# The first stage of a hybrid backbone block: one load of x, one chain for both norms, the shift from two extra columns

## The chip, the cores and the metric

One core of one Trainium2 chip runs the whole block as one program. The metric is device time in microseconds (us), the median of several executions. TensorE (PE) multiplies, VectorE (DVE), ScalarE (ACT) and GpSimd (POOL) do element work, and SyncE (SP) issues most of the loads.

## The reference

A hybrid block over 1024 latent tokens and 256 context tokens of width 1024, one layer deep. What matters for this case is its beginning:

```python
s_lat, s_ctx = jax.nn.silu(c), jax.nn.silu(c_ctx)
mod_l = (s_lat @ w_mod[l] + b_mod[l])[:, None, :]
mod_c = s_ctx @ w_mod[l] + b_mod[l]
sh1, sc1, g1, sh2, sc2, g2 = jnp.split(mod_l, 6, axis=-1)
csh1, csc1, cg1, csh2, csc2, cg2 = jnp.split(mod_c, 6, axis=-1)
u_lat = _modulate(_rmsnorm(x, norm1_g[l]), sh1, sc1)
u_ctx = _modulate(_rmsnorm(ctx, norm1_g[l]), csh1, csc1)
...
rgx_l, rgg_l, mlx_l, mlo_l, gr_l, gm_l = jnp.split(u_lat @ w_in, splits, axis=-1)
xm_l, q_l, k_l, v_l, gin_l = _mlstm_inputs(_to_col_major(mlx_l, rows), ml_conv_w, ml_conv_b, ml_wq, ml_wk, ml_wv)
```

After that come two recurrent branches (RG-LRU and mLSTM, in both directions), a gated merge, a second modulated norm, a SwiGLU and a last norm; none of that is changed.

## The kernel before

The kernel keeps channels on the 128 partitions, so x is eight tiles of 128 x 1024 (channel tile k, all tokens) and the context eight of 128 x 256. Every product with a weight is done in three matmuls, because each factor is split into a high part (`wh`, `ah`) and a low part (`wl`, `al`): wh x ah, wh x al, wl x ah (`gemm`, L106). A weight tile `wr` is loaded by SP; POOL makes `wh` (L94), DVE makes `wl` (L97). For 1024 tokens each matmul comes twice, 512 columns each.

The modulation is a matrix product of its own. `mod_a(i, ...)` multiplies the activated conditioning vector `s` by the tile `wm` number i (L282) and ACT copies the result to `mo` (L285). `mod_b` turns it into columns with `sel` (L292), DVE adds the bias into `modc` (L293), and for tiles 8 to 15, the scale, computes the factor `a1` (L297). Tiles 0 to 7 are the shift.

The first stage, block `p0`, computes the first four output blocks m = 0 to 3 of the part `mlx` of the input projection for the latent tokens. It doesn't wait for the norm. For m = 0 and 1 (the *first pass*) it multiplies x times `a1` without norm and shift: `un_h` and `un_lo` make the two parts of tile k, `part(k, (0, 1))` the 12 matmuls, `un_sq` adds the squares of tile k to `accl`. Then `rms_cols` sums `accl` over the channels (`prms`, L143) and takes the inverse root (`rstd_cols`, L132 to L137, six short operations), and `bcast_col` spreads it over the partitions with PE (`rbl`, L152); the result is `rb`. `put_latent` (L222) copies the accumulators `pg` of blocks 0 and 1 to `X`, POOL multiplies them by `rb` (L445), and ACT adds the shift (L449). The shift's share, `shw`, is the product of the weight with the shift column of `modc`: 16 matmuls of one column (`psh`, L411).

For m = 2 and 3 (the *second pass*) `normed` (L330, L331) makes the normed and shifted tile and `normed_low` (L335) its low part; `part(k, (2, 3))` multiplies. The order of k is 5, 6, 7, 0, 1, 2, 3, 4 here, as five buffers hold x: tiles 5 to 7 are still there, and 0 to 4 are loaded a second time. Within this pass ACT squares the context tiles, POOL adds them up (`accc`, L307), and a second `rms_cols` and `rbc` make the context's norm. DVE then scales the context (L451), ACT makes `ch`, DVE `cl` (L454).

Block `p1` follows: `context(m)` multiplies `ch` and `cl` for block m into `pc`, ACT copies it into `X` ahead of the latent tokens (L510), and DVE runs the convolution over `X`.

All instructions of `p0` on PE, ACT, DVE and POOL stand in a hand-written order: the code's order is the engine's order (`tc.manual_schedule`). SP's loads go out in the order of their calls, at most eight at a time, each when its buffer is free. The order in `p1` is made by a scheduler. `s_s`, the activated conditioning vector, is stored to DRAM by POOL at the start (L232) for use by a row much later (L999); the store writes its 1024 elements one by one.

Of the kernel before, what the change touches and what calls it, by code (L numbers as in the profile page):

```python
# [15 lines left out]
T = 1024  # L16
# [12 lines left out]
MPP = 4  # L29
ENG4 = {mybir.EngineType.PE, mybir.EngineType.Activation, mybir.EngineType.DVE, mybir.EngineType.Pool}  # L30
# [11 lines left out]
def hybrid_block(ctx, tc, xT, ctxT, vec, gbias, wmod, wmt, win, wbr, wbm, wo, wfi, wfo, qkvt, wif, rgw,  # L42
# [160 lines left out]
    ch = uc.tile([128, KT, TC], F32R, name="ch")  # L203
    cl = uc.tile([128, KT, TC], F32R, name="cl")
# [3 lines left out]
    with pool("p1g", bufs=2, space=PSUM) as pg_, pool("p1s", bufs=3, space=PSUM) as ps_, \  # L208
# [15 lines left out]
        with pool("p0") as p0:  # L224
# [7 lines left out]
            nc.gpsimd.dma_start(s_s.rearrange("o (k p) -> p (o k)", p=128), s2[:, :, 0])  # L232
# [10 lines left out]
            x_sb, c_sb = {}, {}  # L243

            def load_mod(*idx):
                for i in idx:
                    wms[i] = p0.tile([128, KT, 128], F32, tag="wm", name="wm", bufs=4)
                    nc.sync.dma_start(wms[i], wmod[i])

            def load_x(k):  # L250
                x_sb[k] = p0.tile([128, T], F32, tag="x", name="x", bufs=5)
                nc.sync.dma_start(x_sb[k], xT[:, k])

            def load_c():
                for j in range(2):
                    t_ = p0.tile([128, KT, 128], F32, tag="wm", name="wm", bufs=4).rearrange("p (a b) c -> p a (b c)", b=2)
                    nc.sync.dma_start(t_, ctxT[:, 4 * j:4 * j + 4])
                    for k in range(4):
                        c_sb[4 * j + k] = t_[:, k]

            accl, sqx = [p0.tile([128, T], F32, name=n) for n in ("accl", "sqx")]
            accc = p0.tile([128, TC], F32, name="accc")
            rb = p0.tile([128, T], F32, name="rb")
            shw = p0.tile([128, 2], F32, name="shw")
# [35 lines left out]
            def ctx_sums():  # L300
                for k in range(KT):
                    if k == 0:
                        nc.scalar.activation(accc, c_sb[0], AF.Square)
                    else:
                        sq = p0.tile([128, TC], F32, tag="sqc", name="sqc", bufs=2)
                        nc.scalar.activation(sq, c_sb[k], AF.Square)
                        nc.gpsimd.tensor_tensor(accc, accc, sq, op=ALU.add)  # L307

            KB = (5, 6, 7, 0, 1, 2, 3, 4)

            def part(k, ms):
                for m in ms:
                    gemm(wfirst[m], halves(pgs[m], uh, ul), [k], *((0, 7) if m < 2 else (KB[0], KB[-1])))

# [7 lines left out]
            def un_sq(k):  # L322
                sq = accl if k == 0 else (rb, sqx)[k % 2]
# [14 lines left out]
            with tc.manual_schedule(engines=ENG4):  # L338
                pgs = [pg_.tile([128, 2, 512], F32, tag="g", name="pg") for _ in range(2)]
# [9 lines left out]
                load_mod(14, 15)  # L349
                un_h(1)  # L350
                un_lo(1)
                wfirst[1][2]()
                un_sq(0)
                load_x(5)
                mod_b(10, 11)
                part(0, (0, 1))
                un_h(2)
                un_lo(2)
                un_sq(1)
                load_x(6)  # L360
                part(1, (0, 1))
# [3 lines left out]
                un_sq(2)  # L365
                load_x(7)
                part(2, (0, 1))
                mod_b(12, 13)
                load_mod(4, 5, 6, 7)
                un_h(4)  # L370
                un_lo(4)
                part(3, (0, 1))
                mod_a(14, 15)
                wfirst.append(load_split(win[18], late=True))
                un_sq(3)
                mod_b(14, 15)
                un_h(5)
                un_lo(5)
                un_sq(4)
                part(4, (0, 1))  # L380
                un_h(6)
                un_lo(6)
                un_sq(5)
                mod_a(4, 5, 6, 7)
                load_mod(0, 1, 2, 3)
                part(5, (0, 1))
# [12 lines left out]
                mod_a(0, 1, 2, 3)  # L399
                load_c()  # L400
# [11 lines left out]
                normed_low(5)  # L412
                normed(6)
                load_x(2)
                normed_low(6)
                load_x(3)
                xs01 = [new_x() for _ in range(2)]
                for m in range(2):
                    put_latent(xs01[m], pgs[m])
                for m in range(2):  # L420
                    pgs.append(pg_.tile([128, 2, 512], F32, tag="g", name="pg"))
                wfirst[3][2]()
                for i, k in enumerate(KB):
                    if i + 2 < KT:
                        normed(KB[i + 2])
                    if i + 1 < KT and i > 0:
                        normed_low(KB[i + 1])
                    if i == 1:
                        load_x(4)
                    if i == 1:  # L430
                        ctx_sums()
                    if i == 0:
                        nc.vector.tensor_copy(shw, psh[:, 0:2])
                    part(k, (2, 3))
                    if i == 3:
                        yc = rms_cols(p0, pc_.tile([128, 512], F32, tag="c", name="prms"), accc, 2)
                    if i == 6:
                        rbc = ps_.tile([128, 512], F32, tag="s", name="rbc")
                        for c in range(2):
                            bcast_col(p0, yc[:, c:c + 1], rbc[:, c * 128:c * 128 + 128])  # L440
                    if i in (1, 3):
                        m = (i - 1) // 2
                        X = xs01[m]
                        xv = X[:, 261:1285].rearrange("p (w r) -> p w r", r=16)
                        nc.gpsimd.tensor_tensor(xv, xv, rb.rearrange("p (r w) -> p w r", r=16), op=ALU.mult)  # L445
                    if i in (5, 6):
                        m = i - 5
                        X = xs01[m]
                        nc.scalar.activation(X[:, 261:1285], X[:, 261:1285], AF.Identity, bias=shw[:, m:m + 1])  # L449
                for k in range(KT):  # L450
                    nc.vector.scalar_tensor_tensor(c_sb[k], c_sb[k], a1[:, k, 1:2], rbc[:, 0:TC], op0=ALU.mult, op1=ALU.mult)  # L451
# [6 lines left out]
        with pool("p1") as p1:  # L458
# [15 lines left out]
            prev = None  # L474

# [1034 lines left out]
```

## Time and profile before

| what | value |
|---|---|
| median of three executions (lowest to highest) | 1910.63 us (1910.33 to 1914.82) |
| the profiled execution's own time | 1913.69 us |
| its span, first to last instruction | 1911.9 us |
| mean granted clock of TensorE | 0.991 |
| PE busy | 1847.2 us, 97% |
| DVE, ACT, POOL busy | 64%, 32%, 18% |
| second pass, first matmul to first context matmul | 72.10 to 105.44 us |

A clock of 1.00 is TensorE's full level, 2.4 GHz, and 0.50 the lower one, 1.2 GHz. A timeline row merges instructions of one kind that follow each other: its start, the time from the first one's start to the last one's end, what they are, and in brackets how long the engine was idle before and whose work ended the idleness. Each fp32 matmul of the modulation, of `psm`, `prms`, `rbl` and `psh` counts as two passes. The DMA share is the mean busy share of 16 DMA engines, and it can pass 1 where several packets of an engine overlap.

### The profile page before, as it was taken

What the parts mean: (1) busy time and instruction counts of PE and PEld (TensorE: products, weight loads), DVE (VectorE), ACT (ScalarE), POOL (GpSimd) and SP (SyncE); (2) the same over time, 40 slices, a digit from 0 to 9 for tenths busy, and PEclk for the clock granted to TensorE, in tenths of its full rate; (3) what the DMA queues carried; (4) which work ended last, traced back from release to release, by engine and by line L of the source; (5) the groups of instructions that cost most, each with busy time, mean ns of one, the idle gap of its engine ahead of it and who ended that gap; (6) DMA issues with size and microseconds to landing.
All of it is one profiled execution on the core that took longest, in us unless ns stands there. A gap on an engine that the chain in (4) does not pass through costs nothing.

```text
span 1911.9 us, 23058 instructions
## 1 busy us (share of the span) xinstructions
PE 1847.2 (97%) x8878; PEld 1520.5 (80%) x8878; DVE 1230.9 (64%) x1887; ACT 610.0 (32%) x842; POOL 348.0 (18%) x452
## 2 busy tenths in 40 slices
PE   6799999999999999999999999999999999999997
PEld 4678778888877878788888888778888888888886
DVE  4676558888716474747776446787755555587755
ACT  3433256767422222222310112443333333210013
POOL 0311111111116151515101013220000000110003
PEclk9899999999999999999999999999999999999998
DMA  9432211212260515150796444343322222653102
GB/s 269 153 141 114 91 53 51 65 50 68 100 187 21 166 25 163 26 162 13 253 346 236 145 150 140 105 143 133 132 85 86 78 83 100 222 176 107 56 1 88
DMA packets 89989, 228.83 MB, mean 120 GB/s; under 512 B 8056, under 2 KB 37272, under 8 KB 89752
## 3 DMA queue, kind: packets, MB, share of 16 engines
q1 hardware_dynamic: 77160, 183.28, 30.0%
q0 software_dynamic: 11888, 43.54, 5.9%
q8 instruction: 70, 1.15, 0.3%
q10 hardware_dynamic: 832, 0.53, 0.1%
q14 instruction: 39, 0.32, 0.1%
HBM read 177.42 MB, written 49.91 MB: 119 GB/s over the span
## 4 chain that ended last, share of the span: by engine, by line
PE 89%; DVE 6%; ACT 1%; DMA 1%; issue 1%; POOL 1%; SPq 0%; DVEq 0%; ACTq 0%
PE pg L110 11%; PE pg L112 11%; PE pg L114 11%; PE pp L1122 7%; PE pp L1124 7%; PE pp L1123 7%; PE pp L1334 4%; PE pp L1336 4%; PE pp L1335 4%; PE po L891 3%; PE pC L896 3%; PE po L889 2%; PE po L110 2%; PE po L112 2%; PE po L114 2%; DMA wm<-in_wmod 1%
## 5 line engine op out<-in xcount | busy, mean ns | idle before, releaser
L110 PE MATMUL pg<-ah,wh 128*128 128x512 f32 x896 | 284.6, 398 | 4.6 <-ACT X L222 3.5
L112 PE MATMUL pg<-al,wh 128*128 128x512 f32 x896 | 282.7, 396 | 5.4 <-DVE al L335 5.4
L114 PE MATMUL pg<-ah,wl 128*128 128x512 f32 x896 | 280.6, 394 | 1.6 <-DVE wl L97 1.6
L94 POOL TENSOR_SCALAR wh<-wr 128x1024 fp32r<-128x1024 f32 x102 | 114.3, 1124 | 597.2 <-PE pg L112 217.5
L97 DVE TENSOR_TENSOR wl<-wr,wh 128x1024 fp32r<-128x1024 f32 x102 | 126.6, 1243 | 120.1 <-POOL wh L94 119.5
L112 PEld LDWEIGHTS pg<-al,wh 128*128 128x128 f32 x896 | 165.4, 190 | 39.9 <-DVE al L335 6.2
L110 PEld LDWEIGHTS pg<-ah,wh 128*128 128x128 f32 x896 | 165.4, 191 | 37.9 <-issue 5.6
L114 PEld LDWEIGHTS pg<-ah,wl 128*128 128x128 f32 x896 | 165.7, 189 | 36.9 <-DVE wl L97 2.0
L1334 PE MATMUL pp<-hh,wh 128*128 128x512 f32 (+1 forms) x384 | 145.1, 378 | 0.0
L1336 PE MATMUL pp<-hh,wl 128*128 128x512 f32 (+1 forms) x384 | 144.8, 377 | 0.0
L1335 PE MATMUL pp<-hh,wh 128*128 128x512 f32 (+1 forms) x384 | 144.8, 377 | 0.0
L1348 DVE SCALAR_TENSOR_TENSOR xs<-pp,g,xs 128x512 f32<-128x512 f32 x144 | 105.3, 746 | 47.8 <-PE pp L1336 43.9
L1122 PE MATMUL pp<-th,oh 128*128 128x512 f32 x264 | 102.8, 389 | 0.0
L1124 PE MATMUL pp<-th,ol 128*128 128x512 f32 x264 | 102.7, 389 | 0.0
L1123 PE MATMUL pp<-tl,oh 128*128 128x512 f32 x264 | 102.7, 389 | 0.0
L1134 DVE TENSOR_TENSOR c<-c,pp 128x512 f32<-128x512 f32 x82 | 56.2, 685 | 69.7 <-PE pp L1124 53.0
L1163 ACT ACTIVATE oh<-os 128x512 fp32r<-128x512 f32 x88 | 55.4, 631 | 130.9 <-PE pp L1123 111.7
L1282 POOL DMA_DIRECT2D s_h<-c x44 | 24.0, 545 | 356.6 <-DVE c L1281 356.6
L1164 DVE TENSOR_TENSOR ol<-os,oh 128x512 fp32r<-128x512 f32 x88 | 60.5, 689 | 39.8 <-ACT oh L1163 39.8
L1334 PEld LDWEIGHTS pp<-hh,wh 128*128 128x128 f32 x384 | 73.1, 190 | 14.0
L1335 PEld LDWEIGHTS pp<-hh,wh 128*128 128x128 f32 x384 | 73.0, 190 | 14.1
L1336 PEld LDWEIGHTS pp<-hh,wl 128*128 128x128 f32 x384 | 73.0, 190 | 13.8
(337 smaller groups left out, 3811.8 us busy)
## 6 DMA issues: line engine op xcount, KB each, us to landing
wr<-in_wfi SPq DMA_DIRECT2D x52, 512.0 KB, 3.3
wr<-in_win SPq DMA_DIRECT2D x48, 512.0 KB, 3.4
wr<-in_wmt SPq DMA_DIRECT2D x32, 512.0 KB, 5.1
s_h<-c POOLq DMA_DIRECT2D x44, 256.0 KB, 2.6
wr<-in_wfo SPq DMA_DIRECT2D x22, 512.0 KB, 3.9
g<-s_h SPq DMA_DIRECT2D x22, 512.0 KB, 4.6
wm<-in_wmod SPq DMA_DIRECT2D x16, 512.0 KB, 6.8
wr<-in_wo SPq DMA_DIRECT2D x16, 512.0 KB, 3.5
```

What stands on the lines that cost most here:

```text
L94: nc.gpsimd.tensor_scalar(h, r, 1.0, 0.0, op0=ALU.mult, op1=ALU.add)
L97: nc.vector.tensor_tensor(l, r, h.bitcast(F32), op=ALU.subtract)
L110: nc.tensor.matmul(o, lhsT=wh[:, k], rhs=h(k), start=f, stop=False)
L112: nc.tensor.matmul(o, lhsT=wh[:, k], rhs=l(k), start=False, stop=False)
L114: nc.tensor.matmul(o, lhsT=wl[:, k], rhs=h(k), start=False, stop=e)
L1122: nc.tensor.matmul(o, lhsT=wh(k), rhs=bh(k), start=new and k == 0, stop=False, skip_group_check=True)
L1123: nc.tensor.matmul(o, lhsT=wh(k), rhs=bl(k), start=False, stop=False, skip_group_check=True)
L1124: nc.tensor.matmul(o, lhsT=wl(k), rhs=bh(k), start=False, stop=not more and k == n - 1, skip_group_check=True)
L1334: nc.tensor.matmul(po, lhsT=wh[:, m], rhs=hh[:, sl], start=i == 0, stop=False)
L1335: nc.tensor.matmul(po, lhsT=wh[:, m], rhs=hl[:, sl], start=False, stop=False)
L1336: nc.tensor.matmul(po, lhsT=wl[:, m], rhs=hh[:, sl], start=False, stop=i == n - 1)
L1348: nc.vector.scalar_tensor_tensor(xs[:, m, sls[t]], po, g2[:, m:m + 1], xs[:, m, sls[t]], op0=ALU.mult, op1=ALU.add)
```

## The change

x is loaded once, into eight buffers. The two context loads go into buffers of their own early in the first pass. Squares of x and of the context go into one accumulator of 1280 columns, and one `rms_cols` of ten columns after part 5 serves both. The shift's share is taken from two more columns of the context product: `ch` and `cl` get 258 columns (`CW`), the last two of which hold the shift. POOL's store of `s_s` moves behind its two products. The second pass takes k in the order 0 to 7, the shift of X is added in `p1`, the modulation 0 to 3 is done ahead of part 6 and 4 to 7 behind part 7. The store for descriptors of software DMAs is set to 4096.

```diff
-    ch = uc.tile([128, KT, TC], F32R, name="ch")
-    cl = uc.tile([128, KT, TC], F32R, name="cl")
+    ch_ = uc.tile([128, KT, CW], F32R, name="ch")
+    cl_ = uc.tile([128, KT, CW], F32R, name="cl")
+    ch, cl = ch_[:, :, 0:TC], cl_[:, :, 0:TC]
...
-            nc.gpsimd.dma_start(s_s.rearrange("o (k p) -> p (o k)", p=128), s2[:, :, 0])
...
-                x_sb[k] = p0.tile([128, T], F32, tag="x", name="x", bufs=5)
+                x_sb[k] = p0.tile([128, T], F32, tag="x", name="x", bufs=8)
...
+            def ctx_sums(j):
+                sq = xs01[j][:, 0:T]
+                nc.scalar.activation(sq, c_t[j].rearrange("p a b -> p (a b)"), AF.Square)
+                nc.vector.tensor_tensor(sq[:, 0:512], sq[:, 0:512], sq[:, 512:1024], op=ALU.add)
...
                 un_h(7)
                 un_lo(7)
-                un_sq(6)
-                un_sq(7)
+                mod_a(0, 1, 2, 3)
+                load_mod(4, 5, 6, 7)
+                wfirst.append(load_split(win[19], late=True))
                 wfirst[2][2]()
-                part(6, (0, 1))
-                mod_b(4, 5, 6, 7)
-                yr = rms_cols(p0, pc_.tile([128, 512], F32, tag="c", name="prms"), accl, 8)
-                load_x(0)
-                load_x(1)
-                wfirst.append(load_split(win[19], late=True))
-                part(7, (0, 1))
-                mod_a(0, 1, 2, 3)
-                load_c()
+                part(6, both)
                 rbl = [ps_.tile([128, 512], F32, tag="s", name="rbl") for _ in range(2)]
...
                 mod_b(0, 1, 2, 3)
-                normed(5)
-                psh = ps_.tile([128, 512], F32, tag="s", name="psh")
-                for m in range(2):
-                    for kk in range(KT):
-                        nc.tensor.matmul(psh[:, m:m + 1], lhsT=wfirst[m][3][:, kk], rhs=modc[:, kk, 0:1], start=kk == 0, stop=kk == KT - 1)
+                rbc = ps_.tile([128, 512], F32, tag="s", name="rbc")
+                for c in range(2):
+                    bcast_col(p0, yr[:, 8 + c:9 + c], rbc[:, c * 128:c * 128 + 128])
+                normed(0)
+                part(7, both)
...
+                normed_low(0)
+                normed(1)
+                mod_a(4, 5, 6, 7)
+                for m in both:
                     put_latent(xs01[m], pgs[m])
...
+                for k in range(KT):
+                    if k + 2 < KT:
+                        normed(k + 2)
+                    if k + 1 < KT:
+                        normed_low(k + 1)
                     part(k, (2, 3))
+                    if k == 0:
+                        mod_b(4, 5, 6, 7)
+                    if k in (0, 3):
+                        xv = xs01[k // 3][:, 261:1285].rearrange("p (w r) -> p w r", r=16)
                         nc.gpsimd.tensor_tensor(xv, xv, rb.rearrange("p (r w) -> p w r", r=16), op=ALU.mult)
-                    if i in (5, 6):
-                        m = i - 5
-                        X = xs01[m]
-                        nc.scalar.activation(X[:, 261:1285], X[:, 261:1285], AF.Identity, bias=shw[:, m:m + 1])
+                    if k + 2 < KT:
+                        nc.vector.scalar_tensor_tensor(c_sb[k + 2], c_sb[k + 2], a1[:, k + 2, 1:2], rbc[:, 0:TC], op0=ALU.mult, op1=ALU.mult)
+                nc.gpsimd.dma_start(s_s.rearrange("o (k p) -> p (o k)", p=128), s2[:, :, 0])
+                sh2 = modc[:, 0:KT, 0:1].to_broadcast([128, KT, 2])
+                nc.scalar.activation(ch_[:, :, TC:CW], sh2, AF.Identity)
+                nc.vector.tensor_tensor(cl_[:, :, TC:CW], sh2, ch_[:, :, TC:CW].bitcast(F32), op=ALU.subtract)
...
-                nc.scalar.activation(X[:, 2:258], pcs.pop(0)[:, 0:TC], AF.Copy)
+                pc = pcs.pop(0)
+                if m < 2:
+                    nc.vector.tensor_copy(shw[:, m:m + 1], pc[:, TC:TC + 1])
+                nc.scalar.activation(X[:, 2:258], pc[:, 0:TC], AF.Copy)
+                if m < 2:
+                    nc.scalar.activation(X[:, 261:1285], X[:, 261:1285], AF.Identity, bias=shw[:, m:m + 1])
...
-    nc = _bacc.Bacc("TRN2", target_bir_lowering=False, num_devices=1)
+    nc = _bacc.Bacc("TRN2", target_bir_lowering=False, num_devices=1, dynamic_dma_scratch_size=4096)
```

The order of instructions changes with it, at three places that the prediction speaks of. The first is POOL's queue from the start to the end of the second pass, first before, then now; `s_77` is the tile of the conditioning vector.

```order
L230 MEMSET s_77 128x256
L232 DMA s_s<-s_77 128x8x1
L94 TENSOR_SCALAR wh<-wr 128x1024 x4
...
L307 TENSOR_TENSOR accc<-accc,sqc 128x256 x7
L445 TENSOR_TENSOR X<-X,rb 128x1024 x2
L560 MEMSET gcol 128x256
```

```order
L232 MEMSET s_77 128x256
L95 TENSOR_SCALAR wh<-wr 128x1024 x4
...
L436 TENSOR_TENSOR X<-X,rb 128x1024 x2
L439 DMA s_s<-s_77 128x8x1
L192 MEMSET X 128x2
```

The store `s_s` stood ahead of the first `wh` and now stands behind the two products; the seven sums `accc` are gone.

The second is PE's queue around the turn from the first pass to the second, first before, then now; the rows `pg` are the matmuls of a part.

```order
L292 MATMUL psm<-sel,mo 128x2 x4
L143 MATMUL prms<-ones,accl 128x1 x8
L110 MATMUL pg<-ah,wh 128x512 x2
L112 MATMUL pg<-al,wh 128x512 x2
L114 MATMUL pg<-ah,wl 128x512 x2
...
L282 MATMUL psmod<-wm,s_77 32x128 x32
L152 MATMUL rbl<-dg,ones 128x128 x8
L292 MATMUL psm<-sel,mo 128x2 x4
L411 MATMUL psh<-modc,wr 128x1 x16
L110 MATMUL pg<-ah,wh 128x512 x2
L112 MATMUL pg<-al,wh 128x512 x2
L114 MATMUL pg<-ah,wl 128x512 x2
```

```order
L144 MATMUL prms<-ones,accl 128x1 x10
L285 MATMUL psmod<-wm,s_77 32x128 x32
L111 MATMUL pg<-ah,wh 128x512 x2
...
L115 MATMUL pg<-ah,wl 128x512 x2
L153 MATMUL rbl<-dg,ones 128x128 x8
L295 MATMUL psm<-sel,mo 128x2 x4
L153 MATMUL rbc<-dg,ones 128x128 x2
L111 MATMUL pg<-ah,wh 128x512 x2
...
L115 MATMUL pg<-ah,wl 128x512 x2
L285 MATMUL psmod<-wm,s_77 32x128 x32
L111 MATMUL pg<-ah,wh 128x512 x2
```

The 16 matmuls `psh` are gone, `rbc` has moved up to `rbl`, and the two modulation groups of 32 stand ahead of part 6 and behind part 7 now, the second one straight ahead of the second pass.

The third is DVE's queue in the second pass, first before (around the second rms chain), then now (its beginning).

```order
L335 SCALAR_TENSOR_TENSOR al<-x,modc,ah 128x1024
L145 TENSOR_SCALAR rmsv<-prms 128x2
L133 RECIPROCAL ry<-ru 128x2
L134 TENSOR_TENSOR ru<-ry 128x2
L135 TENSOR_TENSOR ru<-ru,rmsv 128x2
L136 TENSOR_SCALAR ru<-ru 128x2
L137 TENSOR_TENSOR ry<-ry,ru 128x2
L330 SCALAR_TENSOR_TENSOR x<-x,a_73,rb 128x1024
L335 SCALAR_TENSOR_TENSOR al<-x,modc,ah 128x1024
L330 SCALAR_TENSOR_TENSOR x<-x,a_73,rb 128x1024
```

```order
L338 SCALAR_TENSOR_TENSOR al<-x,modc,ah 128x1024
L296 TENSOR_TENSOR modc<-psm,vt 128x8
L438 SCALAR_TENSOR_TENSOR X<-X,a_73,rbc 128x256
L333 SCALAR_TENSOR_TENSOR x<-x,a_73,rb 128x1024
L338 SCALAR_TENSOR_TENSOR al<-x,modc,ah 128x1024
L438 SCALAR_TENSOR_TENSOR X<-X,a_73,rbc 128x256
L333 SCALAR_TENSOR_TENSOR x<-x,a_73,rb 128x1024
L338 SCALAR_TENSOR_TENSOR al<-x,modc,ah 128x1024
L438 SCALAR_TENSOR_TENSOR c_325<-c_325,a_73,rbc 128x256
L333 SCALAR_TENSOR_TENSOR x<-x,a_73,rb 128x1024
```

The six operations on two columns are gone from this place, and a context product (L438) stands in each round beside the two operations on x.

## Rows read from the trace of the kernel before

**Rows 1.** Page: busy time, share of the span and instructions of each engine.

```profile
PE 1847.2 (97%) x8878; PEld 1520.5 (80%) x8878; DVE 1230.9 (64%) x1887; ACT 610.0 (32%) x842; POOL 348.0 (18%) x452
```

**Rows 2.** Timeline of PE, 5 to 24.5: start, length, instructions, [idle before <- releaser].

```profile
7.00 1.08 PE L282 MATMUL psmod<-wm,s 128*32 128x128 f32 x16 [0.22 <-DMA wm<-in_wmod]
...
19.73 1.08 PE L282 MATMUL psmod<-wm,s 128*32 128x128 f32 x16 [10.13 <-DMA wm<-in_wmod]
20.99 1.08 PE L282 MATMUL psmod<-wm,s 128*32 128x128 f32 x16 [0.19 <-DMA wm<-in_wmod]
22.57 1.01 PE L292 MATMUL psm<-sel,mo 128*128 128x2 f32 x4 [0.50 <-ACT mo L285]
```

**Rows 3.** Timeline of PE, 38 to 73.

```profile
40.10 0.61 PE L292 MATMUL psm<-sel,mo 128*128 128x2 f32 x4 [0.56 <-ACT mo L285]
...
46.41 0.64 PE L282 MATMUL psmod<-wm,s 128*32 128x128 f32 x16 [0.88 <-DMA wm<-in_wmod]
...
64.89 3.70 PE L411 MATMUL psh<-modc,wr 128*128 128x1 f32 x32 [0.35 <-DVE modc L293]
72.10 1.19 PE L110 MATMUL pg<-ah,wh 128*128 128x512 f32 x2 [3.51 <-ACT X L222]
```

**Rows 4.** Timeline of PE, 73 to 120.

```profile
77.94 0.62 PE L110 MATMUL pg<-ah,wh 128*128 128x512 f32 x2
...
80.66 0.62 PE L110 MATMUL pg<-ah,wh 128*128 128x512 f32 x2
...
85.43 0.61 PE L143 MATMUL prms<-ones,accc 128*128 128x1 f32 x4 [0.53 <-POOL accc L307]
...
95.01 1.22 PE L112 MATMUL pg<-al,wh 128*128 128x512 f32 x2 [5.38 <-DVE al L335]
...
105.44 0.28 PE L110 MATMUL pc<-ch,wh 128*128 128x256 f32 x1
106.55 0.39 PE L112 MATMUL pc<-cl,wh 128*128 128x256 f32 x1 [0.83 <-DVE cl L454]
```

**Rows 5.** Stretches: length, busy PE, PEld, DVE, ACT, POOL, PEclk, DMA share, GB/s.

```profile
9.00:18.00 9.00, 0.60 (x3) 0.51 (x3) 0.32 (x2) 1.15 (x1) 0.00 (x0) 1.00 1.26 119
22.00:30.00 8.00, 7.50 (x28) 6.05 (x25) 5.16 (x6) 4.47 (x5) 1.05 (x1) 1.00 1.03 417
...
95.00:100.00 5.00, 4.99 (x13) 3.95 (x14) 4.02 (x5) 3.23 (x3) 0.00 (x0) 0.55 0.00 0
```

**Rows 6.** Timeline of POOL, 3 to 19.

```profile
3.91 1.09 POOL L232 DMA_DIRECT2D s_s<-s  x1 [2.74 <-DVE lpd L167]
```

**Rows 7.** DMA issues from 0 to 130: count, KB each, us to landing.

```profile
qk<-in_qkvt SPq DMA_DIRECT2D x1, 1536.0 KB, 6.7
...
s_s<-s POOLq DMA_DIRECT2D x1, 4.0 KB, 14.1
```

**Rows 8.** Timeline of POOL, 76 to 96.

```profile
85.33 6.82 POOL L445 TENSOR_TENSOR X<-X,rb 128x1024 f32<-128x1024 f32 x2
```

**Rows 9.** Timeline of DVE, 84 to 108.

```profile
87.09 2.26 DVE L134 TENSOR_TENSOR ru<-ry 128x2 f32<-128x2 f32 x1
89.39 2.77 DVE L135 TENSOR_TENSOR ru<-ru,rmsv 128x2 f32<-128x2 f32 x1
...
93.67 1.28 DVE L335 SCALAR_TENSOR_TENSOR al<-x,modc,ah 128x1024 fp32r<-128x1024 f32 x1
94.87 1.28 DVE L330 SCALAR_TENSOR_TENSOR x<-x,a,rb 128x1024 f32<-128x1024 f32 x1
...
98.57 0.47 DVE L151 TENSOR_SCALAR dg<-ident,ry 128x128 f32<-128x128 f32 x2
102.87 3.22 DVE L451 SCALAR_TENSOR_TENSOR wm<-wm,a,rbc 128x256 f32<-128x256 f32 x8 [3.83 <-PE rbc L152]
```

**Rows 10.** Timeline of ACT, 60 to 110.

```profile
70.72 2.35 ACT L222 ACTIVATE X<-pg 128x512 f32<-128x512 f32 x4
```

**Rows 11.** Page: DMA issues over the whole span.

```profile
s_h<-c POOLq DMA_DIRECT2D x44, 256.0 KB, 2.6
```

More of the change, by code (lines that the diff above doesn't have):

```diff
@@ L29 @@
 MPP = 4
+CW = TC + 2
 ENG4 = {mybir.EngineType.PE, mybir.EngineType.Activation, mybir.EngineType.DVE, mybir.EngineType.Pool}
@@ L298, in mod_b @@
                                                    V("n1g", k, n).unsqueeze(2).to_broadcast([128, n, 2]), op0=ALU.add, op1=ALU.mult)
[L300 to L309, printed above, removed]
+            def ctx_sums(j):
+                sq = xs01[j][:, 0:T]
+                nc.scalar.activation(sq, c_t[j].rearrange("p a b -> p (a b)"), AF.Square)
+                nc.vector.tensor_tensor(sq[:, 0:512], sq[:, 0:512], sq[:, 512:1024], op=ALU.add)
+                if j:
+                    nc.vector.tensor_tensor(accc, accc, sq[:, 0:TC], op=ALU.add)
+                    nc.vector.tensor_tensor(accc, accc, sq[:, TC:2 * TC], op=ALU.add)
+                else:
+                    nc.vector.tensor_tensor(accc, sq[:, 0:TC], sq[:, TC:2 * TC], op=ALU.add)
             def part(k, ms):
                 for m in ms:
-                    gemm(wfirst[m], halves(pgs[m], uh, ul), [k], *((0, 7) if m < 2 else (KB[0], KB[-1])))
+                    gemm(wfirst[m], halves(pgs[m], uh, ul), [k])
             def un_h(k):
@@ L338, in hybrid_block @@
             with tc.manual_schedule(engines=ENG4):
-                pgs = [pg_.tile([128, 2, 512], F32, tag="g", name="pg") for _ in range(2)]
+                both = (0, 1)
+                pgs = [pg_.tile([128, 2, 512], F32, tag="g", name="pg") for _ in both]
                 mod_a(8, 9)
@@ L349, in hybrid_block @@
                 load_mod(14, 15)
+                for k in (5, 6, 7):
+                    load_x(k)
+                part(0, (0,))
+                un_sq(0)
                 un_h(1)
+                mod_b(10, 11)
                 un_lo(1)
                 wfirst[1][2]()
[L353 to L356, printed above, removed]
+                part(0, (1,))
+                un_sq(1)
                 un_h(2)
                 un_lo(2)
-                un_sq(1)
-                load_x(6)
-                part(1, (0, 1))
+                part(1, both)
+                un_sq(2)
                 mod_a(12, 13)
@@ L418, in hybrid_block @@
-                for m in range(2):
+                rbc = ps_.tile([128, 512], F32, tag="s", name="rbc")
[3 more added lines that the diff above has]
+                part(7, both)
+                for k in range(2):
+                    nc.vector.scalar_tensor_tensor(c_sb[k], c_sb[k], a1[:, k, 1:2], rbc[:, 0:TC], op0=ALU.mult, op1=ALU.mult)
+                normed_low(0)
+                normed(1)
@@ L419, in hybrid_block @@
+                mod_a(4, 5, 6, 7)
+                for m in both:
                     put_latent(xs01[m], pgs[m])
-                for m in range(2):
-                    pgs.append(pg_.tile([128, 2, 512], F32, tag="g", name="pg"))
+                pgs += [pg_.tile([128, 2, 512], F32, tag="g", name="pg") for _ in range(2)]
                 wfirst[3][2]()
[L423 to L433, printed above, removed]
-                    part(k, (2, 3))
[L435 to L442, printed above, removed]
-                        X = xs01[m]
-                        xv = X[:, 261:1285].rearrange("p (w r) -> p w r", r=16)
-                        nc.gpsimd.tensor_tensor(xv, xv, rb.rearrange("p (r w) -> p w r", r=16), op=ALU.mult)
-                    if i in (5, 6):
-                        m = i - 5
-                        X = xs01[m]
-                        nc.scalar.activation(X[:, 261:1285], X[:, 261:1285], AF.Identity, bias=shw[:, m:m + 1])
@@ L474, in hybrid_block @@
             prev = None
+            shw = p1.tile([128, 2], F32, name="shw")
             def small_mats():
```

60 lines of the change are left out of this document (31 added, 29 removed).

## Prediction

> **What bounds the kernel now.** I read the busy row first: TensorE (PE) is busy 97% of the span [rows 1], so a gain can come only from the few places where PE stands idle or runs at the lower of its two clock levels, and the change touches the beginning, up to the convolutions. So PE's row-by-row timeline of the beginning came next, and each bracket there is a wait. Four matter: 10.13 us until the load of modulation weights 10 arrives [rows 2]; 3.51 us until ACT has emptied the accumulators of blocks 0 and 1 [rows 3]; 5.38 us until VectorE (DVE) delivers a low part `al`; 0.83 us for `cl` [rows 4]. Add 3.70 us of `psh` matmuls, 16 of them with one column each (the row counts 32 passes) [rows 3], and stretches at clock 0.55, that is mostly at 1.2 GHz instead of 2.4 [rows 5]. I walked the new instruction order through this stretch with durations of the old rows.
>
> **Term 1, the start: -9.0 us.** Why does the load take that long? The second modulation tile had landed at 7.0 [rows 2]. Four 512 KB loads later (x0, first wr, modulation 10 and 11) PE goes on at 20.99. In the stretch 22 to 30 the loads run at 417 GB/s, 1.26 us each; in 9 to 18 they make 119 GB/s although the DMA engines are fully occupied (share 1.26) [rows 5]. In that stretch lies `s_s`, 1024 elements of 4 bytes that POOL issues at 3.91 [rows 6] and that land 14.1 us later, at 18.0 [rows 7]; at 19.73 PE has its data. The change moves this store behind the POOL products `X*rb`. I take it to be the cause: 7.0 + 4 x 1.26 = 12.0 instead of 20.99, so -9.0. Bounds: 0, if the loads are slow on their own, to -9.0.
> In the new place: the second pass should begin at 72.10 - 9.0 - 3.5 = 59.6 and end near 85.6 (terms below); the products take 6.82 [rows 8], so the store goes out near 66 and is down near 80. SP's next load, `qk`, waits for the last DVE work of this part, behind 85. So nothing loads beside the store: 0. Bounds: 0, as in a stretch without loads (95 to 100 has DMA share 0.00 [rows 5]), and, if store and load did meet, 9.0 as at the start less what hides: `qk` needs 6.7 us to land [rows 7], PE first has context products, so some 6. I take 0, whose row is nearer.
> The Trainium skill ("DMA: Bandwidth & Descriptors", Specifications) states that transfers below 512 B are read-modify-write and miss line rate. The trace agrees for the store itself (14.1 us for 4 KB); that other queues suffer from it the page doesn't say, and by the page alone the term would be 0, which is rival A's time.
>
> **Term 2, from modulation 11 to the second pass (20.99 to 72.10): -3.5 us.** Gone from PE's path: `psh`, 3.70 and its wait 0.35 (the shift now comes out of two extra context columns, 258 instead of 256, under 1% of two context products: nothing); ACT's 3.51; the modulation wait 0.88, since modulation 0..3 and 4..7 have more work ahead of them; two waits for `mo` of 0.50 and 0.56 [rows 2, 3], since a gemm part now stands between product and use. Sum 9.50. One `psm` group moves into the second pass and `rbc` out of it, both stay on PE's path: 0. The five x reloads also go; PE's waits name none of them, so 0.
> New on the path: (a) DVE does al0, modc, a1, al1 and then the low part wl17, which PE's block 1 of part 0 needs: one DVE pass more, 1.2 [rows 9] (0 to 2.4); (b) the sums of squares end just before `prms`, now ahead of psmod and part 6 instead of part 7: 0 to 2.4 (two DVE passes), I take 1.0; (c) `rbl` and `rbc` have less PE work ahead of them while DVE makes ten `dg` tiles of 0.24 each [rows 9] (0, all hidden, to 2.4): 0.85; (d) the accumulators: on ACT the four copies, 2.35 [rows 10], stand behind two `ah` and `mo`, and PE has the 12 matmuls of part 7 and psmod to do meanwhile; between 1.2 (two copies alone) and 3.5 (as now), I take 2.7; (e) two more `prms` columns, at most the 0.61 that two take now [rows 4], 0.25. Sum 6.0; 6.0 - 9.5 = -3.5. Ends: all low 1.45, so -8.0; all high 11.3, so +1.8.
>
> **Term 3, second pass (72.10 to 105.44): -7.3 us.** Gone: the 5.38 wait [rows 4]. Its making: the two-column rms chain on DVE, where one 128x2 operation took 2.26 us and the next 2.77 [rows 9] during POOL's two products, 6.82 us [rows 8]. The chain leaves this pass. With it go the wait for POOL's sums 0.53 and `prms` 0.61 [rows 4], and the low clock that follows the stall: 13 matmuls took 4.99 us, 0.384 each [rows 5], where 12 undisturbed ones take 2.72 (77.94 to 80.66 [rows 4]), 0.227 each, so 13 x 0.157 = 2.0. Sum 8.6. New: DVE, which per k now does normed, low part and a context product, 1.20 + 1.20 [rows 9] + 3.22 / 8 = 0.40, so 2.80, against PE's 2.72 for 12 matmuls: 8 x 0.08 = 0.6, plus 0.7 for the part of a POOL product that falls beside DVE work: 1.3. Bounds of this last: 0.6 if POOL never disturbs, 6.1 if both products (2.77 each as DVE saw one) stand fully in DVE's way.
>
> **Term 4, contexts: +0.4.** The `cl` wait of 0.83 [rows 4] goes, as its first factor is done inside the pass. The shift copy on DVE must read `pc` before the single `pc` buffer is free: 2 x 0.25 (by `dg`, 0.24); behind it DVE works on the first convolution, so the second copy may come up to one convolution pass later: 0.7. Bounds -0.8 to +2.5. The X shift itself (ACT, about 1.2 per block by the four copies of half a block in 2.35 [rows 10]) moves from the pass to behind the context product; the next context product covers it on PE; without cover it would cost 2.4.
> The smaller descriptor store and the seven adds that POOL loses I cost at nothing: POOL is 18% busy [rows 1].
>
> **Sum:** -9.0 - 3.5 - 7.3 + 0.4 = -19.4. The profiled execution took 1913.69 (span 1911.9), about 3 more than the median 1910.63; the difference is a plain offset, so it is taken off the median: **1891.2 us**.
>
> **Rival A, the loads stay slow.** Term 1 is 0 because the loads are slow there on their own. For it: nothing but the coincidence in time speaks for `s_s`. Against it: 417 GB/s at 22, when more loads are asked for, and the collapse ends when `s_s` lands. 1910.63 - 10.4 = **1900.2**.
>
> **Rival B, POOL and DVE take turns.** The products now are issued at once, at k = 0, where DVE makes normed and low parts that PE waits for. The mechanism is there now [rows 8, 9]: a 128x2 operation lasts as long as a POOL product leaves it waiting (2.26 and 2.77), while a larger `dg` right after POOL's end takes 0.24. Both products in the way: +5.5 instead of the 1.3 taken, so 4.2 lost: 1891.2 + 4.2 = **1895.4**. Against: DVE waits for `psm` of 4..7 behind the first part there, so one product falls into idle time.
> The Trainium skill ("SBUF — State Buffer", Who interferes with whom) has the rule that a DVE instruction with two SBUF inputs and a POOL instruction that reads SBUF exclude each other for a whole instruction. By that rule the trace agrees (2.26 and 2.77 us), and all of normed and low parts, with two SBUF inputs each, would be subject to it.
>
> **Rival C, slower: the descriptor store.** It is set to 4096 now. If a POOL store must wait until an earlier one has landed, POOL's queue stands, and the `wh` casts behind it, which PE needs, are late. The largest group is 44 stores of 256 KB, 2.6 us to landing [rows 11]. It decides from 19.4 / 44 = 0.44 us per store on PE's path; at 0.65 each it adds 28.6: 1891.2 + 28.6 = about **1920**. Against: these stores wait for DVE, not for each other, and POOL idles 82%.
>
> **How the numbers follow.** Forecast 0.63, with its own range 1885.5 to 1896 (terms 2 to 4 at their partial ends); A 0.12, B 0.18, C 0.05; that the savings are filled elsewhere, so no change, 0.02. The range 1884 to 1901 holds 0.92 of the forecast, nearly all of B and a little over half of A: 0.58 + 0.17 + 0.07 = 0.82. 0.3% is 5.7 us, about what this kernel's measurement can tell. Faster by more than that: forecast, A and B, 0.93, less 0.01 for their tails, 0.92; within it 0.04 (those tails, the case of no change and the small end of C); slower 0.04 (the rest of C).
>
> **What would show it.** Right: the third modulation wait ends near 12, no stretch with full DMA share and 119 GB/s there, and that stretch returns harmlessly between 60 and 86; no wait over 3 us on PE after it; the second pass takes 26 us instead of 33.34; first context some 20 us earlier. Wrong: the modulation wait still ends near 20 (A); DVE's normed or low parts of 2.5 us and more and PE waiting on `al` (B); POOL rows of stores followed by late `wh` in the feed-forward part (C); a `qk` landing over 10 us.

## The result: 1889.0 us, 1.15% faster

The changed kernel takes 1888.99 us (median of 5 runs, 1888.54 to 1891.56) against 1910.63 (median of 5 runs, 1910.33 to 1914.82) for the kernel before. The ratio is 0.9885, 95% interval 0.9871 to 0.9899. Forecast were 1891.2 us and a range of 1884 to 1901. The profiled execution has a span of 1887.1 us.

The beginning of the changed kernel, PE's timeline from 5 to 24.5 (start, length, instructions, idle time before and whose work ended it):

```profile
10.98 1.08 PE L285 MATMUL psmod<-wm,s 128*32 128x128 f32 x16 [1.21 <-DMA wm<-in_wmod]
12.25 1.08 PE L285 MATMUL psmod<-wm,s 128*32 128x128 f32 x16 [0.18 <-DMA wm<-in_wmod]
...
19.55 0.91 PE L115 MATMUL pg<-ah,wl 128*128 128x512 f32 x2 [1.77 <-DVE wl L98]
```

Against [rows 2] the wait for modulation 10 has fallen from 10.13 to 1.21, and modulation 11 starts at 12.25 instead of 20.99. A wait of 1.77 for the low part `wl` of the second weight tile is new. In the stretches (length, busy PE, PEld, DVE, ACT, POOL, PEclk, DMA share, GB/s), the first answers to [rows 5] and the second is what follows that wait:

```profile
9.00:18.00 9.00, 7.38 (x50) 5.29 (x50) 4.58 (x7) 5.28 (x6) 2.09 (x2) 1.00 1.03 417
19.50:24.00 4.50, 4.45 (x13) 3.50 (x14) 3.46 (x3) 0.00 (x0) 0.00 (x0) 0.62 1.02 407
62.00:86.40 24.40, 23.34 (x104) 18.61 (x105) 20.25 (x27) 12.24 (x19) 6.99 (x6) 1.00 0.02 1
```

The loads run at 417 GB/s where they ran at 119. After the new wait the clock is 0.62, and 13 matmuls take 4.45 us. The third stretch, the whole second pass, is at clock 1.00. PE's timeline from 56 to 110 shows its start, its one wait, and the first context product; the rows answer to [rows 3, 4]:

```profile
58.11 1.96 PE L285 MATMUL psmod<-wm,s 128*32 128x128 f32 x64
61.98 0.70 PE L111 MATMUL pg<-ah,wh 128*128 128x512 f32 x2 [1.92 <-issue]
...
70.13 0.74 PE L113 MATMUL pg<-al,wh 128*128 128x512 f32 x2 [1.06 <-DVE al L338]
...
86.40 0.28 PE L111 MATMUL pc<-ch,wh 128*128 128x258 f32 x1
...
90.11 0.39 PE L111 MATMUL pc<-ch,wh 128*128 128x258 f32 x1 [0.67 <-ACT X L507]
```

The waits of 3.51, 5.38 and 0.83 are gone; 1.92 (labelled "issue", so with no releaser in the profile), 1.06 and 0.67 stand in their places. What the 1.06 is made of is in POOL's and DVE's timelines of that time:

```profile
61.96 5.84 POOL L436 TENSOR_TENSOR X<-X,rb 128x1024 f32<-128x1024 f32 x2 [9.03 <-ACT X L224]
67.74 1.09 POOL L439 DMA_DIRECT2D s_s<-s  x1
```

```profile
65.82 0.17 DVE L296 TENSOR_TENSOR modc<-psm,vt 128x8 f32<-128x8 f32 x1 [4.32 <-PE psm L295]
...
66.29 2.60 DVE L333 SCALAR_TENSOR_TENSOR x<-x,a,rb 128x1024 f32<-128x1024 f32 x1
68.81 1.27 DVE L338 SCALAR_TENSOR_TENSOR al<-x,modc,ah 128x1024 fp32r<-128x1024 f32 x1
...
70.40 1.27 DVE L333 SCALAR_TENSOR_TENSOR x<-x,a,rb 128x1024 f32<-128x1024 f32 x1
```

One `normed` takes 2.60 us while POOL's second product is still at work (until 67.8); the next takes 1.27. In a second profile of the same kernel this `normed` takes 1.76 us and PE's wait is 0.22, so the 1.06 is one execution's size. The store `s_s` goes out at 67.74 and lands 9.6 us later, with nothing loading beside it; `qk` takes 6.5 us to land, as before (6.7 in [rows 7]).

Taken at four marks of PE's work, the forecast and the profiles give (the last column is by the second profile of the changed kernel, whose marks are 12.67, 61.18, 86.04 and 201.22):

| term | marks in the trace, before and after | forecast | measured | second profile |
|---|---|---|---|---|
| 1, start | modulation 11 begins: 20.99, 12.25 | -9.0 | -8.7 | -8.3 |
| 2, to the second pass | it begins: 72.10, 61.98 | -3.5 | -1.4 | -2.6 |
| 3, second pass | first context product: 105.44, 86.40 | -7.3 | -8.9 | -8.5 |
| 4, contexts | first matmul of the gate rows: 223.10, 201.59 | +0.4 | -2.5 | -2.5 |
| sum | | -19.4 | -21.5 | -21.9 |

The last mark is in the two timelines of PE, first before, then after:

```profile
223.10 0.74 PE L558 MATMUL pgr<-gsel,gacc 128*128 128x16 f32 x6
```

```profile
201.59 0.74 PE L557 MATMUL pgr<-gsel,gacc 128*128 128x16 f32 x6
```

The spans differ by 24.8, 3.3 more than at that mark. The second profile (below) bears on what that is.

### The profile page after: what moved, and what is told of

It is laid out like the page before. It is cut to its first block, busy times and chain, and to the rows that moved or that the text cites. A ratio compares the mean times of both kernels' runs of the same rounds, so it can differ in the third digit from the quotient of the medians.

```text
span 1887.1 us, 22965 instructions
## 1 busy us (share of the span) xinstructions
PE 1842.4 (98%) x8846; PEld 1516.9 (80%) x8846; DVE 1224.3 (65%) x1888; ACT 609.4 (32%) x836; POOL 340.9 (18%) x445
## 3 DMA queue, kind: packets, MB, share of 16 engines
q8 instruction: 70, 1.15, 0.2%
## 4 chain that ended last, share of the span: by engine, by line
PE 92%; DVE 5%; ACT 1%; issue 1%; DMA 0%; POOL 0%; SPq 0%; DVEq 0%; ACTq 0%
PE pg L111 12%; PE pg L113 12%; PE pg L115 12%; PE pp L1121 7%; PE pp L1123 7%; PE pp L1122 7%; PE pp L1333 4%; PE pp L1335 4%; PE pp L1334 4%; PE po L890 3%; PE pC L895 3%; PE po L888 2%; PE po L111 2%; PE po L113 2%; PE po L115 2%; PE pt L700 1%
```

## The experiments

Runs of one group shared their chip with runs of the kernel before, and each ratio is to these. The changed kernel stood at 0.9885 (0.9871 to 0.9899) and, in its second measurement, at 0.9888 (0.9873 to 0.9903).

### The store s_s alone, both ways

```diff
-            nc.gpsimd.dma_start(s_s.rearrange("o (k p) -> p (o k)", p=128), s2[:, :, 0])
...
                         nc.gpsimd.tensor_tensor(xv, xv, rb.rearrange("p (r w) -> p w r", r=16), op=ALU.mult)
+                    if i == 3:
+                        nc.gpsimd.dma_start(s_s.rearrange("o (k p) -> p (o k)", p=128), s2[:, :, 0])
```

> The kernel before with one edit: POOL's store s_s goes out behind the second product X*rb instead of ahead of the first wh. Theory (the store holds up the loads while it is in flight): the wait for modulation 10 ends near 12 instead of 19.73, the loads run at about 400 GB/s from 9 to 18, psmod of 11 starts near 12.2 as in the changed kernel, and the time falls by 6 to 9 us. Rival A (the loads are slow there on their own): the wait still ends near 20 and the time stays within 1 us. A third case: the start gains 9 us but the second pass waits for x reloads that now come too late; then under 5 us.

And the reverse, in the changed kernel:

```diff
             nc.vector.tensor_scalar(s2[:, :, 0:2], t.rearrange("p (a b) -> p a b", b=2), 0.5, None, op0=ALU.mult)
+            nc.gpsimd.dma_start(s_s.rearrange("o (k p) -> p (o k)", p=128), s2[:, :, 0])
...
-                nc.gpsimd.dma_start(s_s.rearrange("o (k p) -> p (o k)", p=128), s2[:, :, 0])
```

> The changed kernel with the store s_s back at the start, ahead of the first wh. Theory (store holds up the loads): the wait for modulation 10 ends near 20 instead of 10.98 and about 8 us of the gain are lost, 1897 instead of 1889. Rival A: no difference within 1 us.

Moved late, the kernel before takes 1904.58, ratio 0.9954 (0.9941 to 0.9966), 8 us faster. Moved back, the changed kernel takes 1897.85, ratio 0.9927 (0.9915 to 0.9939), 7 to 9 us slower than in its two measurements. The stretch 9 to 18 of the one and of the other, columns as above:

```profile
9.00:18.00 9.00, 6.13 (x45) 4.69 (x46) 4.69 (x5) 3.54 (x5) 2.09 (x2) 1.00 1.02 411
```

```profile
9.00:18.00 9.00, 1.01 (x4) 0.93 (x4) 2.74 (x4) 1.18 (x2) 1.04 (x1) 1.00 1.06 135
```

The store's place alone decides between 411 and 135 GB/s. It is the loads' own packets that last longer: those of 4 KB take 0.16 us each from 9 to 18 in the trace of the changed kernel, and 0.65 on average and up to 6.3 in that of the kernel before. With nothing loading the store lands in 9.4 to 11.4 us over all runs, beside the first loads in 12.8 to 14.9. Both theories held and rival A falls: the gate rows begin 8.0 us earlier than in the kernel before with the store moved late (215.12 for 223.10), and 8.0 later than in the changed kernel with it moved back (209.58 for 201.59). No run changed the store's form, so that its elements of 4 bytes are to blame, and not that it is a store of POOL's queue, is argued and not shown.

### The descriptor store

```diff
-    nc = _bacc.Bacc("TRN2", target_bir_lowering=False, num_devices=1)
+    nc = _bacc.Bacc("TRN2", target_bir_lowering=False, num_devices=1, dynamic_dma_scratch_size=4096)
```

> The kernel before with the store for software DMA descriptors set to 4096 and nothing else. Theory: it only frees room, 0 within 1.5 us. Rival C: POOL's stores wait for one another, more than 0.3 us for each of the 44 stores s_h, so 13 us or more slower.

1913.88 us, ratio 1.0003 (0.9993 to 1.0012): no difference. Rival C falls. The changed kernel was not run with the larger store; that the eight x buffers need the room is not shown by a run.

### The 16 matmuls psh

```diff
-                psh = ps_.tile([128, 512], F32, tag="s", name="psh")
-                for m in range(2):
-                    for kk in range(KT):
-                        nc.tensor.matmul(psh[:, m:m + 1], lhsT=wfirst[m][3][:, kk], rhs=modc[:, kk, 0:1], start=kk == 0, stop=kk == KT - 1)
...
-                        nc.vector.tensor_copy(shw, psh[:, 0:2])
+                        nc.vector.tensor_copy(shw, modc[:, 0, 0:2])
```

> The kernel before without the 16 matmuls psh: the shift of X in blocks 0 and 1 is another column instead of the product, so that part is left out. By the prediction's sum psh and its wait are time of their own: 4.05 us faster. Rival: ACT's copies X<-pg end last there (they start at 70.72 behind two ah that wait for DVE), so PE's wait before 72.10 grows from 3.51 to about 7.5 and the time stays within 1 us.

1912.72 us, ratio 0.9995 (0.9986 to 1.0003): nothing, as the rival said. PE's timeline shows why, as the wait has grown from 3.51 to 7.56:

```profile
63.12 0.95 PE L292 MATMUL psm<-sel,mo 128*128 128x2 f32 x8
71.64 1.19 PE L110 MATMUL pg<-ah,wh 128*128 128x512 f32 x2 [7.56 <-ACT X L222]
```

`psh` and the wait behind it were one gap whose end ACT set. Taking `psh` out is worth nothing while ACT's copies stand where they do. The other half of the gap was tried by putting the copies first:

```diff
+                xs01 = [new_x() for _ in range(2)]
+                for m in range(2):
+                    put_latent(xs01[m], pgs[m])
                 mod_b(0, 1, 2, 3)
                 normed(5)
...
-                xs01 = [new_x() for _ in range(2)]
-                for m in range(2):
-                    put_latent(xs01[m], pgs[m])
```

> The kernel before with the four copies X<-pg ahead of the modulation columns 0 to 3 and of normed(5) and normed(6), psh unchanged. Theory (psh and the wait behind it are one gap whose end ACT sets, as the copies stand behind two ah): PE goes on right after psh, the wait of 3.51 falls below 0.7, the time falls by 2.8 to 3.5 us, and now psh is what is left of the gap. Rival (the copies are late for another reason, or the low part of tile 5 then comes late): under 1 us.

1910.72 us, ratio 0.9992 (0.9983 to 1.0001): under what the runs can tell, and a miss against the 2.8 to 3.5 of the theory. In PE's timeline the wait is gone, the second pass starts at 68.92 right behind `psh` (at low clock 5.07 us long now), but PE waits 2.92 instead of 0.53 for POOL's sums `accc` later on:

```profile
63.98 5.07 PE L414 MATMUL psh<-modc,wr 128*128 128x1 f32 x32 [0.35 <-DVE modc L293]
68.92 1.20 PE L110 MATMUL pg<-ah,wh 128*128 128x512 f32 x2
...
85.02 0.61 PE L143 MATMUL prms<-ones,accc 128*128 128x1 f32 x4 [2.92 <-POOL accc L307]
...
88.93 1.22 PE L112 MATMUL pg<-al,wh 128*128 128x512 f32 x2 [2.73 <-DVE al L335]
```

The sums did not move (85.02 against 85.43 in [rows 4]): in ACT's timelines the squares stand behind two `ah` that wait for DVE's `normed`, at 74.12 here and 74.50 in the kernel before. With 2.73 and 0.67 for `al`, where it was 5.38, the pass waits 6.3 us instead of 5.9. So a second bound stood right behind the first. Counted from the first gemm matmul (22.53 here, 23.45 before), the second pass starts 2.3 us earlier, and 1.5 of it are left at the first context product; the change moves both bounds.

### POOL's products

In either kernel the two products are cut to 128 of 1024 columns:

```diff
-                        nc.gpsimd.tensor_tensor(xv, xv, rb.rearrange("p (r w) -> p w r", r=16), op=ALU.mult)
+                        nc.gpsimd.tensor_tensor(xv[:, 0:8], xv[:, 0:8], rb.rearrange("p (r w) -> p w r", r=16)[:, 0:8], op=ALU.mult)
```

> The kernel before with each of POOL's two products X*rb cut to 128 of 1024 columns; the rest of X stays unscaled. Theory (POOL's product keeps DVE's two-column operations waiting): L134 and L135 take about 0.2 us each instead of 2.26 and 2.77, the wait of 5.38 falls below 1, the low clock after it goes, and the time falls by 5 to 7.5 us. Rival (the wait has another cause, the chain of dependences DVE-ACT-DVE): the wait stays over 3 us and the time falls by less than 2.

> The changed kernel with each of POOL's two products X*rb cut to 128 of 1024 columns; the rest of X stays unscaled. Theory: one normed of 2.60 us at 66.29 falls to 1.28 and PE's wait of 1.06 at 70.13 goes, so about 1 us faster and no more, since DVE feeds the pass at 2.8 us per k. Rival B (both products stand in DVE's way): 4 us or more faster.

In the kernel before: 1904.71 us, ratio 0.9958 (0.9946 to 0.9971), 8 us faster by the medians and 7.2 at the gate rows (215.90 for 223.10), so the theory held. DVE's chain, and PE's wait behind it, in their timelines:

```profile
86.56 0.34 DVE L134 TENSOR_TENSOR ru<-ry 128x2 f32<-128x2 f32 x1
86.93 0.16 DVE L135 TENSOR_TENSOR ru<-ru,rmsv 128x2 f32<-128x2 f32 x1
```

```profile
89.94 0.73 PE L112 MATMUL pg<-al,wh 128*128 128x512 f32 x2 [0.86 <-DVE al L335]
```

The two operations take 0.34 and 0.16 us instead of 2.26 and 2.77 [rows 9], and the wait is 0.86 instead of 5.38. In the changed kernel the same cut gives 1889.46 us, ratio 0.9886 (0.9873 to 0.99), no difference to the changed kernel; in its trace `normed` falls from 2.60 to 1.28, the wait of 1.06 is gone, and from the first gemm matmul to the first `psG` matmul it takes 78.7 us instead of 79.8 (79.1 in the second profile). So rival B's mechanism is there, at 0.4 to 1.1 us of the 5.5 it could cost.

### PE's waits in the changed kernel

Three order edits: the copies ahead of `mo`, `wl17` ahead of `modc` and `al1`, and `rbc` ahead of `psm` of 0 to 3. The first and the second were also run alone, the third was not.

```diff
+                wfirst[1][2]()
                 mod_b(10, 11)
                 un_lo(1)
-                wfirst[1][2]()
...
-                mod_b(0, 1, 2, 3)
                 rbc = ps_.tile([128, 512], F32, tag="s", name="rbc")
...
+                mod_b(0, 1, 2, 3)
...
-                mod_a(4, 5, 6, 7)
                 for m in both:
                     put_latent(xs01[m], pgs[m])
+                mod_a(4, 5, 6, 7)
```

> The changed kernel with ACT's four copies X<-pg ahead of the copy mo of modulation 4 to 7. Theory: PE's gap of 1.92 before the second pass (61.98) comes from the copies standing behind mo; it falls to about 0.4, 1.5 us faster. Rival: the gap moves, since psm of 4 to 7 now waits for a later mo or DVE's al comes late; within 0.5 us of the changed kernel.

> The changed kernel with one edit: DVE's low part wl17 ahead of modc and al1. Theory: the wait of 1.77 at 19.55 and the low clock behind it go, prms comes 2.5 to 3.3 us earlier; the time falls by about 2.5 us. Rival: the later waits (rbc, the copies) give it back, under 1 us.

> The changed kernel with three edits of order: the copies ahead of mo (as in the run with that alone), DVE's low part wl17 ahead of modc and al1, and the two rbc columns ahead of psm of 0 to 3. Theory, by the waits of the changed kernel's profile: 1.5 for the copies, 1.77 plus about 1.5 of low clock behind it for wl17, 1.27 for rbc: 4 to 6 us faster, near 1884. Rival: DVE paces the second pass at 2.8 us per k, so what is won ahead of it is given back there: under 2 us.

| run | median us | ratio (95%) |
|---|---|---|
| copies ahead of `mo` | 1890.17 | 0.9891 (0.9876 to 0.9906) |
| `wl17` ahead | 1887.55 | 0.9873 (0.9856 to 0.9889) |
| all three | 1887.24 | 0.9871 (0.9858 to 0.9885) |

The copies alone bring nothing in time, as the rival had it; PE's gap is 1.86 and not the 0.4 of the theory. `wl17` ahead removes the wait: `prms` starts 23.66 behind the first gemm matmul instead of 26.27 (14.53 to 38.19, and 13.26 to 39.53 in the changed kernel), 2.6 us for a wait of 1.77 (2.3 against the second profile), and the row of `pg<-ah,wl` has no bracket and no low clock behind it:

```profile
18.92 0.63 PE L115 MATMUL pg<-ah,wl 128*128 128x512 f32 x2
...
20.45 0.63 PE L115 MATMUL pg<-ah,wl 128*128 128x512 f32 x2
```

The time falls by 1.4 to 3.4 us by the medians of the two measurements of the changed kernel; the intervals overlap, so in time it is likely and not shown. In the traces the gate rows begin at 199.04 with `wl17` ahead and at 198.07 with all three, against 201.59 and 201.22 in the two profiles of the unedited kernel. All three together are no better in time than `wl17` alone, 1.8 to 3.7 us by the medians, under the 4 to 6 of the theory. PE's gap before the second pass did not shrink with them; it is 2.50 in the run with `wl17` alone, 2.74 with all three, and 3.27 in the second profile of the unedited changed kernel, where part 7 happened to run at full clock:

```profile
55.95 1.95 PE L285 MATMUL psmod<-wm,s 128*32 128x128 f32 x64
61.18 1.19 PE L111 MATMUL pg<-ah,wh 128*128 128x512 f32 x2 [3.27 <-issue]
```

The gap ends with ACT's copies. In ACT's timeline of the changed kernel they stand behind an `ah` that waits for DVE's `normed(1)`, and in this execution behind a `mo` that waits for PE as well:

```profile
58.00 1.15 ACT L334 ACTIVATE ah<-x,modc 128x1024 fp32r<-128x1024 f32 x1 [2.55 <-DVE x L333]
60.13 0.60 ACT L288 ACTIVATE mo<-psmod 128x512 f32<-128x512 f32 x1 [0.98 <-PE psmod L285]
60.62 2.38 ACT L224 ACTIVATE X<-pg 128x512 f32<-128x512 f32 x4
```

PE starts the second pass 1.33 to 1.36 us behind the first copy, when two of the four are done, in both profiles of the unedited kernel and in the three runs of the table (copies from 60.62, 59.83, 59.25, 57.66 and 56.17, PE from 61.98, 61.18, 60.58, 59.00 and 57.50), whatever PE does ahead of it. In all five that `ah` waits 2.55 us for `normed(1)`. Hence a last order, with the copies ahead of `normed(1)` as well:

```diff
-                normed(1)
-                mod_a(4, 5, 6, 7)
                 for m in both:
                     put_latent(xs01[m], pgs[m])
+                normed(1)
+                mod_a(4, 5, 6, 7)
```

> The changed kernel with the order edits of the run with three, but the four copies X<-pg now stand ahead of normed(1) on ACT, so not behind an ah that waits for DVE. Theory (PE's gap before the second pass, 2.74 in the run with three, is ACT waiting for that ah): the gap falls below 0.5 and the low clock behind it goes, some 3 to 4 us faster than the run with three, near 1884. Rival: DVE paces the second pass at 2.8 us per k and al of k = 1 comes later behind the later ah, so PE waits there instead; within 1 us of the run with three (1887.2).

1889.68 us, ratio 0.9880 (0.9867 to 0.9894): a miss, and the clearest sight of rival B. PE starts the second pass at 55.19 without any wait, and then stops:

```profile
55.19 0.73 PE L111 MATMUL pg<-ah,wh 128*128 128x512 f32 x2
...
62.14 1.22 PE L115 MATMUL pg<-ah,wl 128*128 128x512 f32 x2 [4.39 <-DVE wl L98]
```

```profile
54.28 6.73 POOL L436 TENSOR_TENSOR X<-X,rb 128x1024 f32<-128x1024 f32 x2 [1.30 <-ACT X L224]
```

```profile
54.28 4.01 DVE L333 SCALAR_TENSOR_TENSOR x<-x,a,rb 128x1024 f32<-128x1024 f32 x1
58.22 3.87 DVE L98 TENSOR_TENSOR wl<-wr,wh 128x1024 fp32r<-128x1024 f32 x1
62.01 1.27 DVE L333 SCALAR_TENSOR_TENSOR x<-x,a,rb 128x1024 f32<-128x1024 f32 x1
```

With the copies early POOL's products are early as well, and DVE's `normed` and `wl` take 4.01 and 3.87 us beside them instead of 1.28 and 1.22. That is 5.4 us of lock, the price given to rival B, and PE's wait of 4.39 is its end. In the changed kernel the late copies put the products into a stretch where DVE waits 4.32 us for `psm`: the late start hides them.

### The second profile of the changed kernel

> The changed kernel once more, on the chip of the next run, for a second profile. If the 1.8 us between the row work (494) and the mLSTM loop (574) and the 1.5 us after 1650 that the first pair of profiles shows are differences between executions, they differ again here by as much; if they belong to the change, the profile repeats to 0.3 us there. Time 1889 within 2 us.

1890.92 us, ratio 0.9888 (0.9873 to 0.9903). Beyond the beginning, the first pair of profiles differs by 1.8 us between 494 and 574 and by 1.5 behind 1650. In the first of these stretches the second profile repeats the first to 0.1 us, which by the expectation would speak for the change; but the runs without `psh` and with the small descriptor store, whose code there is that of the kernel before, take 1.7 and 1.9 less than its profile between 494 and 574, so that profile of the kernel before was long there. The 1.5 did not come again: the second profile takes 1.5 more than the first behind 1624, and 1.4 more between 550 and 838. So single executions of the same code differ by as much, and of the 24.8 between the spans about 21.5 belong to the change, which is what the medians give (21.6; 21.0 in the second measurement).

## Why the prediction was right, and where it was not

The causes that it named for terms 1 and 3, which make up most of the gain, held. That the total came so near (-21.5 for -19.4) is in part luck: term 2 fell short by 2.1, and terms 3 and 4 gave 1.6 and 2.9 more than forecast.

Term 1 held: the store was the cause, -8.7 for -9.0, and both directions of the edit give 8 us. What spoke for it was the landing at 18.0 just ahead of the end of the wait; it was an inference from coincidence, and the two runs are what shows it. The Trainium skill ("DMA: Bandwidth & Descriptors", Specifications) has a rule on transfers below 512 B; it speaks of the rate of the transfer itself, and these runs show the larger cost, the two thirds of their rate (135 GB/s for 411) that the loads of another queue lose.

Term 3 held in its cause: the two-column chain beside POOL's products. Its size was off by 1.6 (-8.9 for -7.3). The sum counted the low clock behind the stall of 5.38 and left out that at the old pass's start, in the stretches of the kernel before:

```profile
72.00:76.00 4.00, 3.90 (x10) 3.11 (x11) 4.00 (x6) 2.45 (x4) 0.00 (x0) 0.54 0.88 294
```

10 matmuls in 3.90 us, 0.39 each instead of 0.227, are 1.6 us; in the profile after, the pass is at clock 1.00 from its start. The split between terms 2 and 3 hangs on that: in the second profile the pass starts 0.8 earlier (61.18), at low clock, and the first `psG` matmul comes within 0.4 of the first profile (92.74 for 93.09).

Term 2 is the mis-sized term: -1.4 for -3.5 (-2.6 in the second profile). The new waits came out at 1.77 (`wl17`, forecast 1.2), 0.79 (sums, 1.0), 1.27 (`dg`, 0.85) and 1.92 (copies, 2.7): 5.75 for 5.75. That the sum is met is luck, as each is off by 0.2 to 0.8, and in the second profile they are 1.77, 0.79, 0.54 and 3.27, together 6.37. What failed is that each was priced as its idle time alone. The run with `wl17` ahead shows 2.3 to 2.6 us for the wait of 1.77, as the clock is 0.62 behind it. Over the whole of term 2, PE worked at the lower clock for 9.8 us in the kernel before, for 14.5 after and for 10.3 in the second profile. Two matmuls of 512 columns start every 0.85 us there and every 0.47 at full clock, so about 45% of that time is lost: 4.4, 6.5 and 4.6 us, an estimate from these rows. The 2.1 more are what is missing in the first profile; in the second it is 0.2 of low clock and 0.6 of longer waits. And the sum took `psh` and the 3.51 behind it as two savings; the run without `psh` shows that they were one gap with ACT at its end. As both went, the sum is not wrong for it, but the reason given for each was.

Term 4 had the wrong sign: -2.5 for +0.4. PE's waits between the first context product and the gate rows fell from 2.8 (0.83 `cl`, 0.94 for `pc`, 1.08 for a `wh` that the sum had not listed) to 1.0; the shift copy on DVE added 0.2 to the first `pc` wait (0.67 for 0.47) and not 1.2 in all; the first copy found DVE idle. The remaining 0.7 is PE's busy time and not explained.

Rival B was put right in size: the sum took 0.7 us for POOL's products beside DVE and 0.6 for DVE's pace; the first came to 1.06 (0.22 in the second profile), and no wait shows the second. The rule of the Trainium skill ("SBUF — State Buffer", Who interferes with whom), that a DVE instruction with two SBUF inputs and a POOL instruction that reads SBUF exclude each other for a whole instruction, agrees with all three traces (2.26 and 2.77; 2.60; 4.01 and 3.87). It was the timing that kept it small, as the last order shows. Two of the signs that the prediction named for being wrong did show, without the loss that they stood for: a `normed` over 2.5 us with PE waiting on `al` (2.60 and 1.06), and, in the second profile, a PE wait over 3 us (3.27).

## What to carry to other kernels

Look for stores of single elements among the first instructions: one of 4 KB cost 8 us because it held up the loads beside it, and moving it is one line. A wait that follows a piece of work on the same engine may belong to it: ask who ends the gap, take the piece out, and see if the wait grows by it. Before an engine's work is moved earlier, look at what it sets off: here earlier copies set off POOL's products in DVE's way and gave nearly all of the gain back (1889.68 us, for 1887.24 with the later copies).

## What the runs showed that was not expected

A casting operation of POOL holds DVE up as the products do. POOL's and DVE's timelines of the changed kernel with short products show a `wh` and, beside it, a `normed` of 2.06 us instead of 1.28:

```profile
52.62 1.10 POOL L95 TENSOR_SCALAR wh<-wr 128x1024 fp32r<-128x1024 f32 x1 [18.16 <-DVE dg L152]
```

```profile
52.73 2.06 DVE L333 SCALAR_TENSOR_TENSOR x<-x,a,rb 128x1024 f32<-128x1024 f32 x1
...
59.54 1.28 DVE L333 SCALAR_TENSOR_TENSOR x<-x,a,rb 128x1024 f32<-128x1024 f32 x1
```

In the run with `wl17` alone it is the other way round: there the `normed` begins first (51.10, 1.28 us), and the `wh` at 51.17 takes 2.13 us instead of 1.05. A wait of term 2 may hold some of this: in the first profile of the changed kernel the two `dg` tiles for `rbc` take 1.07 us beside a `wh` and PE waits 1.27 for them, in the second they take 0.47 and PE waits 0.54; no run tried it.

The same 12 matmuls of part 7 ran mostly at low clock in one execution of the changed kernel and at full clock in the next (4.5 us and 3.0 until `psmod`), with nearly the same end of the gap behind them: the time that PE wins there is handed to the wait.
